# A normalisation, a projection and a state-space mixer whose instructions follow one order listed in the source

## The chip, the cores and the metric

The kernel runs on one NeuronCore of a Trainium2 chip. The core has five engines with a queue each: TensorE (PE in the profile), VectorE (DVE), ScalarE (ACT), GpSimd (POOL) and SyncE (SP), which here only starts transfers. An engine takes its instructions strictly in the order of its queue and stops at one whose inputs are not there yet. Transfers are started from SP, ACT and POOL. The metric is the device time of the whole kernel in microseconds (us); the median of the runs of a kernel is compared.

## The reference

The reference is a trunk of two layers on a sequence of 1024 vectors of 1024 elements (one sequence). Layer 0 mixes along the sequence with a diagonal state-space mixer (S5), layer 1 with a Mamba-2 mixer, and each mixer is followed by a squared-ReLU MLP. All is float32. Only the beginning of layer 0 is touched by the change:

```python
mod = cond @ ada_w[i] + ada_b[i]                   # cond = silu(c)
sh1, sc1, g1, sh2, sc2, g2 = jnp.split(mod[:, None, :], N_MOD, axis=-1)
h = _modulate(_rmsnorm(x, norm_mix_g[i]), sh1, sc1)   # norm * (1 + scale) + shift
# inside _s5_mixer:
u = (h @ w_in).astype(f32)                         # 1024 x 1024 by 1024 x 1024
bu = jnp.einsum('btgh,gph->btgp', u_blk, b_bar)    # 64 groups of 16 channels, 64 complex states
_, hs = lax.associative_scan(_s5_combine, (a_elems, bu), axis=1)
y = jnp.einsum('btgp,ghp->btgh', hs, c_mat).real
g = jax.nn.gelu(y + d * u)
val, gate = jnp.split(g @ w_glu + b_glu, 2, axis=-1)
x = x + g1 * (val * jax.nn.sigmoid(gate))
```

## The kernel before

Activations lie transposed: eight tiles of 128 channels (index k or m), each in two halves of 512 positions (index f). A float32 product in full precision is made of three float32r products (`mm3`, lines 118 to 120): of the high part of the weight with the high and the low part of the activation, and of the low part of the weight with the high part of the activation. So each weight unit of 128x1024 is loaded by SP into a tile `raw`, its high part is cast by ACT (`whi`, L85) and its low part is the difference, made by DVE (`wlo`, L86).

The part that the change touches is the first 270 us or so, in three steps.

**The first norm.** Eight loads bring x. ACT squares each half tile (`sq`, L196), PE sums the squares over channels in four strips of 32 rows of a bank (L184), DVE makes the inverse root (`rsqrt`). The scale is eight weighted sums on DVE (L403, each over a loaded tile `ada`), the shift is a product on PE (L381: one row of 512, eight terms after each other, for each half of the channels), which ACT copies out (L351), PE turns into columns (L354) and DVE stores as `mod` (L386). Then DVE scales each half tile (L1655), ACT adds the shift and rounds (L244) and DVE makes the low part (L245). Beside it DVE computes tables of powers and phases for the mixer (`s5_tables`).

**The input projection** (`s5_uproj`) makes u in eight blocks m of 128 channels, each in two halves. ACT copies each out to a tile `us` (L1098) in another order of positions, and for six of the eight blocks ACT writes it to DRAM and SP loads it back as the tile U (L1148). Blocks 6 and 7 go from `us` to U by eight transfers of 64 KB each (L1146).

**The mixer** works through the same eight blocks; a block is eight groups, worked in two quads (16 quads in all, called q below). `s5_front` and `s5_back` build the matrices of a block: DVE forms ET and Fa (L981, three instructions each per quad); PE makes the taps of a short convolution (L1028), which ACT copies into `kp`; POOL writes them skewed to DRAM by eight transfers (L1043) and loads them back as M (L1060), which ACT reorders (`Mp`, L1062); two transfers from POOL make Fb, which is Fa with its two halves of the partitions exchanged (L1065, L1066); PE transposes ET (L1073) and ACT copies it out as E; ACT and DVE make phases and ACT their sines (`si`, `co`, L1079 to L1088, with L1080 and L1081 on DVE). `s5_main` then takes a quad: PE multiplies U by E into two banks p1 and p2 (L1155, L1156); DVE turns them by the phase (three instructions, L1138), scans along the sequence (four, L1163) and turns back by two products, qa and qb (L1138); PE sums U by M, qa by Fa and qb by Fb in one bank (L1175, L1177); ACT applies GELU (`gy`, L1181) and starts its transfer to DRAM. `s5_gather` loads the result in tiles by channel and splits them into high and low parts (L1204, L1205). The gated linear unit (`glu`) takes these as its input; its first products are made while the mixer's last quads still run, and its first activation is `gt` (L1230).

The order on each engine is not written in the source: a scheduler orders the instructions by a priority, from the order of the program, and by a cost model, before the kernel runs. Tiles come from rings of buffers, and an instruction that takes a buffer waits until its last reader is done.

Of the kernel before, what the change touches and what calls it, by code (L numbers as in the profile page):

```python
# [19 lines left out]
P = 128  # L20
# [5 lines left out]
DIRECT = (6, 7)  # L26
# [156 lines left out]
def strip(K, bank, col, rows, k):  # L183
    K.nc.tensor.matmul(  # L184
        bank[blk(k % 4, 32)], col.to_broadcast([P, 32]), rows, start=k < 4, stop=k >= KT - 4, skip_group_check=True
    )


def rstd_first(K, x):

    nc = K.nc
    pr = [psw(K), psw(K)]
    for k in range(KT):
        for f in range(2):
            sq = tmp(K, "sq")
            nc.scalar.activation(sq, x[k][f], AF.Square)  # L196
            strip(K, pr[f], K.ones, sq, k)
    pt = columns(K, pr, K.heads)
    v = K.tmp.tile([P, 8], F32, tag="rfv", name="rfv")
    nc.vector.tensor_scalar(v, pt[:, 0:8], 1.0 / D, EPS, op0=ALU.mult, op1=ALU.add)  # L200
    y = K.tmp.tile([P, 8], F32, tag="rfy", name="rfy")
    rsqrt(K, y, v)
    return [spread(K, y[:, f * 4:f * 4 + 4], psw) for f in range(2)]
# [99 lines left out]
def mod_setup(K):  # L303
    nc = K.nc
    cc, tc = K.tmp.tile([P, 8], F32, tag="cc", name="cc"), K.tmp.tile([P, 8], F32, tag="ct", name="ct")
    nc.scalar.dma_start(cc, K.io.ccol)
    nc.scalar.activation(tc, cc, AF.Tanh, scale=0.5)
    K.condc = K.const.tile([P, 8], F32, name="condc")
    nc.vector.scalar_tensor_tensor(K.condc, tc, 1.0, cc, op0=ALU.add, op1=ALU.mult)
    K.mod = K.const.tile([P, 96], F32, name="mod")  # L310
    K.G = K.const.tile([P, 32], F32, name="G")

# [31 lines left out]
def columns(K, rows, heads=None):  # L344

    nc = K.nc
    pt = pss(K)
    for f, r in enumerate(rows):
        row = tmp(K, "row")
        n = P if heads else 1  # L350
        nc.scalar.copy(row[0:n], r[0:n])  # L351
        for j in range(4):
            o = pt[:, f * 4 + j:f * 4 + j + 1]
            nc.tensor.matmul(o, row[0:n, blk(j)], heads or K.ones[0:1], start=True, stop=True)  # L354
    return pt


def mod_first(K, units):


    nc, V, io = K.nc, K.nc.vector, K.io

    def tile():
        return K.adap.tile([P, 1024], F32, tag="ada", name="ada", bufs=K.nada)

    def blocks(f):
        ts = [tile().rearrange("p (k c) -> p k c", k=2) for _ in range(4)]
        for j, t in enumerate(ts):
            nc.sync.dma_start(t, io.ada0[2 * j:2 * j + 2, :, half_of(f)].rearrange("k p c -> p k c"))
        return ts  # L370

    def rows(f):
        ts = [tile() for _ in range(4)]
        for j, t in enumerate(ts):
            nc.sync.dma_start(t, io.ada[0, 8 + f * 4 + j])
        return ts

    def shift(f, ts):
        pr = pss(K)
        for k in range(KT):  # L380
            nc.tensor.matmul(  # L381
                pr[0:1], K.condc[:, k:k + 1], ts[k // 2][:, k % 2], start=k == 0, stop=k == KT - 1
            )
        pt = columns(K, [pr])
        o = C_ADAB + f * 4
        V.scalar_tensor_tensor(  # L386
# [3 lines left out]
    first = blocks(0), rows(0)  # L390
    units()
    gb, gh = [K.tmp.tile([P, 8], F32, tag=t, name=t, bufs=1) for t in ("fgb", "fgh")]
    g0 = K.cst[:, C_GMIX:C_GMIX + 8]
    V.scalar_tensor_tensor(gb, K.cst[:, C_ADAB + 8:C_ADAB + 16], 1.0, g0, op0=ALU.add, op1=ALU.mult)
    V.tensor_scalar(gh, g0, 0.5, None, op0=ALU.mult)
    acc = K.tmp.tile([P, 8], F32, tag="mac0", name="mac0", bufs=1)
    for f in range(2):
        bs, rs = (blocks(1), rows(1)) if f else first
        shift(f, bs)
        for j, r in enumerate(rs):  # L400
            k = f * 4 + j
            a = acc[:, k:k + 1]
            V.scalar_tensor_tensor(r, r, 1.0, K.cond, op0=ALU.mult, op1=ALU.mult, accum_out=a)  # L403
            nc.scalar.activation(
                K.G[:, k:k + 1], a, AF.Identity, scale=gh[:, k:k + 1], bias=gb[:, k:k + 1]
            )
            yield k
# [452 lines left out]
def s5_tables(K, keep, pool, Lm):  # L860
# [25 lines left out]
    V.memset(S.quarter, TWO_PI / 4)  # L886

# [4 lines left out]
    m1, em1 = exp_acc(K, pool, a, 64, minus_one=True)  # L892

# [34 lines left out]
    )  # L928
    S.R = []
    for nm in "12":  # L930
        r = keep.tile([P, 64, 9], F32, name="R" + nm, tag="R" + nm, bufs=1)
        u = pool.tile([P, 64, 9], F32, name="su", tag="su", bufs=1)
        sines(K, r, ph, *o[nm], u)
        V.tensor_tensor(r, r, mag, op=ALU.mult)
        S.R.append(r)

# [10 lines left out]
    V.tensor_tensor(s2, s2, s2, op=ALU.mult)  # L947
    V.tensor_tensor(s2, s2, m1, op=ALU.mult)
    V.scalar_tensor_tensor(nr, s2, -2.0, em1, op0=ALU.mult, op1=ALU.add)
    V.tensor_tensor(ni, ni, m1, op=ALU.mult)  # L950
    den, t = T("den"), T("dent")
    V.tensor_tensor(den, re, re, op=ALU.mult)
    V.tensor_tensor(t, im, im, op=ALU.mult)
    V.tensor_tensor(den, den, t, op=ALU.add)
# [17 lines left out]
    return S  # L972


def s5_front(K, S, pool, outp, m):


    nc, V, io = K.nc, K.nc.vector, K.io
# [951 lines left out]
```

## Time and profile before

| what | value |
|---|---|
| median of 3 runs | 2464.45 us (2461.76 to 2466.18) |
| the profiled execution | 2460.05 us |
| its span | 2458.3 us |
| busy share of the span: PE, DVE, ACT, POOL | 97%, 77%, 48%, 10% |
| start of the last GELU of the mixer | 258.52 us |
| start of the first activation of the gated unit (`gt`) | 271.26 us |

In the profile an engine's busy time is the time in which at least one of its instructions ran; idle time stands with what ended it. Instructions of one engine overlap by a little: the next one starts before the last one is over, so what an instruction costs its engine is the distance from start to start, and this is shorter than its duration. A line number is that of the kernel before unless the text says otherwise. The change ends with the first part of the gated unit: from there to the end both kernels have the same instructions in the same order on each engine.

### The profile page before, as it was taken

What the parts mean: (1) busy time and instruction counts of PE and PEld (TensorE: products, weight loads), DVE (VectorE), ACT (ScalarE), POOL (GpSimd) and SP (SyncE); (2) the same over time, 40 slices, a digit from 0 to 9 for tenths busy, and PEclk for the clock granted to TensorE, in tenths of its full rate; (3) what the DMA queues carried; (4) which work ended last, traced back from release to release, by engine and by line L of the source; (5) the groups of instructions that cost most, each with busy time, mean ns of one, the idle gap of its engine ahead of it and who ended that gap; (6) DMA issues with size and microseconds to landing.
All of it is one profiled execution on the core that took longest, in us unless ns stands there. A gap on an engine that the chain in (4) does not pass through costs nothing.

```text
span 2458.3 us, 32615 instructions
## 1 busy us (share of the span) xinstructions
PE 2396.3 (97%) x11496; PEld 1941.5 (79%) x11496; DVE 1893.7 (77%) x3205; ACT 1173.9 (48%) x1999; POOL 250.9 (10%) x468
## 2 busy tenths in 40 slices
PE   7899999999999899999999999999999999999997
PEld 2688888888788688878877777877888888888886
DVE  6998755968878997867695867789688788687665
ACT  4688313744444344534564655534147444454442
POOL 0232000122221000000000000000011222210000
PEclk9999999999999999999999999999999999999998
DMA  7566861567869999723454554674236677694752
GB/s 259 156 192 166 285 212 60 193 205 267 278 218 354 322 320 314 252 86 130 138 163 152 159 167 144 185 245 139 88 125 201 223 243 258 246 327 159 262 191 87
DMA packets 286260, 502.23 MB, mean 204 GB/s; under 512 B 23345, under 2 KB 163153, under 8 KB 286097
## 3 DMA queue, kind: packets, MB, share of 16 engines
q1 hardware_dynamic: 242336, 384.64, 49.0%
q0 software_dynamic: 33536, 107.90, 12.4%
q10 hardware_dynamic: 10224, 7.62, 1.0%
q8 instruction: 90, 1.47, 0.2%
q14 instruction: 74, 0.60, 0.1%
HBM read 362.71 MB, written 131.60 MB: 201 GB/s over the span
## 4 chain that ended last, share of the span: by engine, by line
PE 71%; issue 12%; DMA 6%; DVE 6%; ACT 3%; POOL 2%; DVEq 0%; SPq 0%; POOLq 0%; ACTq 0%
PE pd L119 8%; PE pd L118 8%; PE pd L120 8%; PE py L119 4%; PE py L120 4%; PE py L118 4%; PE px L118 3%; PE px L119 3%; PE px L120 3%; PE pv L118 2%; PE pv L119 2%; PE pv L120 2%; DMA ada<-in_ada 2%; PE pm L118 2%; PE pm L120 2%
## 5 line engine op out<-in xcount | busy, mean ns | idle before, releaser
L85 ACT CAST whi<-raw 128x1024 fp32r<-128x1024 f32 x241 | 251.3, 1048 | 417.6 <-PE pd L119 142.6
L86 DVE TENSOR_TENSOR wlo<-raw,whi 128x1024 fp32r<-128x1024 f32 x241 | 293.3, 1218 | 127.0 <-ACT whi L85 123.5
L341 DVE SCALAR_TENSOR_TENSOR ada<-ada,cond 128x1024 f32<-128x1024 f32 x80 | 97.5, 1223 | 44.1 <-DMA ada<-in_ada 43.9
L434 POOL DMA_DIRECT2D hscr<-x x32 | 17.4, 542 | 952.3 <-DVE x L815 753.5
L542 ACT ACTIVATE s<-s 128x512 f32<-128x512 f32 x84 | 53.1, 633 | 96.8 <-DVE s L540 95.3
L1361 DVE SCALAR_TENSOR_TENSOR cacc<-cr,conv,cacc 128x1024 f32<-128x1024 f32 x72 | 91.9, 1280 | 0.8 <-ACT cacc L1342 0.6
L1414 ACT ACTIVATE L<-csb,cs 128x128 f32<-128x128 f32 x224 | 69.9, 391 | 40.9 <-DMA csb<-csr 40.8
L549 POOL DMA_DIRECT2D b<-s x96 | 51.9, 541 | 277.8 <-ACT s L543 263.8
L549 POOL DMA_DIRECT2D b<-tt x96 | 51.9, 541 | 34.1 <-DVE tt L554 24.2
L543 ACT ACTIVATE s<-s 128x512 f32<-128x512 f32 x84 | 53.2, 633 | 2.7
L540 DVE TENSOR_TENSOR s<-s,px 128x512 f32<-128x512 f32 x60 | 40.9, 681 | 16.7 <-PE px L120 16.7
L1365 ACT ACTIVATE cth<-cacc 128x512 f32<-128x512 f32 x48 | 27.7, 625 | 42.0 <-DVE cacc L1361 40.0
L730 DVE SCALAR_TENSOR_TENSOR x<-py,mod,x 128x512 f32<-128x512 f32 x40 | 27.8, 746 | 23.6 <-PE py L120 23.6
L1043 POOL DMA_DIRECT2D kscr<-kp x64 | 34.4, 546 | 99.9 <-ACT kp L1034 98.4
L1230 ACT ACTIVATE gt<-pd,bgh 128x512 f32<-128x512 f32 x16 | 11.0, 686 | 67.9 <-PE pd L120 40.1
L118 PE MATMUL pd<-h00h,whi 128*128 128x512 f32 (+1 forms) x97 | 39.8, 412 | 2.8 <-ACT whi L85 2.8
L1434 DVE SCALAR_TENSOR_TENSOR y<-xs,cst,pm 128x128 f32<-128x128 f32 x128 | 38.3, 342 | 4.8 <-PE pm L1431 4.8
L1341 ACT COPY cr<-pd 128x512 f32<-128x512 f32 x48 | 27.8, 580 | 28.5 <-PE pd L120 28.5
L120 PE MATMUL pd<-h00h,wlo 128*128 128x512 f32 (+1 forms) x97 | 38.6, 398 | 2.8 <-DVE wlo L86 2.8
L215 ACT ACTIVATE sq<-x 128x512 f32<-128x512 f32 x28 | 16.8, 625 | 50.6 <-DVE x L730 45.6
L118 PE MATMUL pd<-h01h,whi 128*128 128x512 f32 x97 | 39.5, 408 | 0.8 <-DVE h61h L815 0.6
L554 DVE TENSOR_TENSOR tt<-s,b 128x512 f32<-128x512 f32 x56 | 38.6, 690 | 0.8
(1017 smaller groups left out, 8122.7 us busy)
## 6 DMA issues: line engine op xcount, KB each, us to landing
raw<-in_w SPq DMA_DIRECT2D x204, 512.0 KB, 4.8
br<-b SPq DMA_DIRECT2D x112, 512.0 KB, 5.7
ada<-in_ada SPq DMA_DIRECT2D x96, 512.0 KB, 5.0
b<-s POOLq DMA_DIRECT2D x96, 256.0 KB, 4.5
b<-tt POOLq DMA_DIRECT2D x96, 256.0 KB, 4.8
csb<-csr SPq DMA_DIRECT2D x32, 512.0 KB, 4.6
raw<-in_w_xbc SPq DMA_DIRECT2D x24, 512.0 KB, 4.3
xscr<-cacc SPq DMA_DIRECT2D x24, 512.0 KB, 2.7
```

Of the source, the lines that this page charges most:

```text
L85: K.nc.scalar.copy(hi, src)
L86: K.nc.vector.tensor_tensor(lo, src, hi.bitcast(F32), op=ALU.subtract)
L118: K.nc.tensor.matmul(ps, wh, xh, start=start and i == 0, stop=False, skip_group_check=more)
L119: K.nc.tensor.matmul(ps, wh, xl, start=False, stop=False, skip_group_check=more)
L120: K.nc.tensor.matmul(ps, wl, xh, start=False, stop=stop and i == n - 1, skip_group_check=more)
L341: K.nc.vector.scalar_tensor_tensor(r, r, 1.0, K.cond, op0=ALU.mult, op1=ALU.mult, accum_out=acc)
L540: nc.vector.tensor_tensor(t, t, p, op=ALU.add)
L542: nc.scalar.activation(t, t, AF.Relu)
L543: nc.scalar.activation(t, t, AF.Square)
L549: self.K.nc.gpsimd.dma_start(self.bscr[DOWN.index(nm)][m // 2][m % 2], t)
L1361: V.scalar_tensor_tensor(acc, cr[:, t:t + L], K.cw[:, i, t:t + 1], acc, op0=ALU.mult, op1=ALU.add)
L1414: nc.scalar.activation(Lm[:, r, :], cb[:, r, :], AF.Relu, bias=S.cs[:, c0 + r:c0 + r + 1], scale=-1.0)
```

## The change

The text of the program for these three steps is cut into some 600 small steps with names such as `A.3` (the product of U and E for quad 3), and a table in the source lists them in one order. Inside that stretch the scheduler is told to keep the order in which the steps are written, on all five engines. So each engine's queue is the list with the other engines' steps left out. Besides:

- The sums of squares and the shift's product both go through four strips of 32 columns and are summed by a product with a column that has a one at the head of each strip (`Strips`). Before, the shift's product was one row of 512.
- The products of the power table with the magnitudes, and the small chain that makes the tables q, move from DVE to POOL; qx moves from DVE to ACT.
- The rounding of the phase (L1080 on DVE) becomes a second run of eight activations on ACT with a bias (`pk`).
- The diagonal term is made once on POOL, and added to the taps by one small instruction of POOL per block (`tap0`). ACT copies all eight taps.
- Instead of Fb and a product with it, qb is added to qa with its two halves of partitions exchanged by two transfers from POOL that accumulate (`added`), and one product with Fa follows. Block 7 keeps Fa, Fb and two products, with Fb made by SP.
- U is filled straight from `us` for all blocks, by eight transfers from SP; DRAM is no longer used for it. The skewed writes of the taps, the loading back of M, the writes of the GELU's result and half of the last quads' transfers move to SP.
- Three of the gathered tiles are loaded into buffers of the mixer that have become free.

```diff
+ORDER = """
+x.0 lam cst x.3 x.7 x.6 cr tb.0 x.4 sq.0.1 tb.1 sq.0.0 x.1 sq.7.0 cc cnd rw.1.2 sq.3.0 x.5 tb.2 x.2 sq.6.0
...
+Fx.5 hi.4 sw.1 Ex.4 Fy.4 ul.2.0 T.3 ia.3 Fy.5 ml.1 Fz.4 To.3 Fz.5 pr.3.1.0 tp.4 tp.5 cd.2 ou.0 to.4 Ey.4 lo.4
+ib.3 to.5 sn.2 Ez.4 bc.4 pr.3.0.1 Ex.5 A.3 ic.3 pk.2 t0.2 Ey.5 ph.2 cx.2 fi.3 pr.3.1.1 cy.2 B.1 ca.3 di.1 tu.2
...
+class Strips:
+    def add(self, col, rows, strip):
+        n = self.n[strip] = self.n.get(strip, 0) + 1
+        self.K.nc.tensor.matmul(
+            self.bank[blk(strip, 32)], col.to_broadcast([P, 32]), rows, start=n == 1, stop=n == 2,
+            skip_group_check=True,
+        )
...
+    for r in S.R:
+        G.tensor_tensor(r, r, mag, op=ALU.mult)
...
+    def tap0(self, m):
+        kp = self.o[m].kp
+        self.nc.gpsimd.tensor_tensor(kp[:, :, 0], kp[:, :, 0], self.S.dI[:, 2 * m:2 * m + 2], op=ALU.add)
...
+    def skew(self, m):
+        for g in range(8):
...
+            self.nc.sync.dma_start(skew, src.unsqueeze(1).to_broadcast([16, 8, 128]))
...
+    def U(self, m, half):
...
+        for g in range(half * 4, half * 4 + 4):
+            self.nc.sync.dma_start(b.U[:, g], us[blk(g, 16)])
...
+    def added(self, q):
+        qa, qb = self.r["q", q]
+        for i in range(2):
+            self.nc.gpsimd.dma_start(qa[blk(i, 64)], qb[blk(1 - i, 64)], accum_op=ALU.add)
...
+        pairs = ((b.Fa, qa), (b.Fb, qb)) if m in TWO else ((b.Fa, qa),)
...
+    order = tc.manual_schedule(engines={E.PE, E.DVE, E.Activation, E.SP, E.Pool})
+    order.__enter__()
...
+    for step in ORDER.split():
+        name, *args = step.split(".")
+        do[name](*map(int, args))
+    order.__exit__(None, None, None)
```

In the table, `sn` is the scan of a quad, `cx` and `cy` are the two products that turn back, `sw` the two accumulating transfers, `B` the products into the bank that the GELU (`ou`) reads; `ul` fills half of a U, `sk` writes and `ml` loads the taps, `pr` is half of a projection's products.

How the queues move, first DVE in the norm. `mod` is the shift's columns, `ada` the weighted sums of the scale, `rfv` the start of the inverse root. Before:

```order
L403 SCALAR_TENSOR_TENSOR ada,mac_546<-ada,cond 128x1024 x2
L1655 SCALAR_TENSOR_TENSOR x_213<-x_213,G,pm 128x512
L1655 SCALAR_TENSOR_TENSOR x_214<-x_214,G,pm 128x512
L386 SCALAR_TENSOR_TENSOR mod<-pn,cst 128x4
L403 SCALAR_TENSOR_TENSOR ada,mac_546<-ada,cond 128x1024
L245 SCALAR_TENSOR_TENSOR h00l<-x_213,mod,h00h 128x512
```

and in the changed kernel:

```order
L467 SCALAR_TENSOR_TENSOR ada,mac_254<-ada,cond 128x1024 x3
L1018 TENSOR_SCALAR phik<-rt 128x64
L1019 TENSOR_SCALAR phik<-phik 128x64
L1020 SCALAR_TENSOR_TENSOR phi<-rt,phik 128x64
L1833 SCALAR_TENSOR_TENSOR x_215<-x_215,G,pm 128x512
L1833 SCALAR_TENSOR_TENSOR x_216<-x_216,G,pm 128x512
L1833 SCALAR_TENSOR_TENSOR x_213<-x_213,G,pm 128x512
L1833 SCALAR_TENSOR_TENSOR x_216<-x_216,G,pm 128x512
L1833 SCALAR_TENSOR_TENSOR x_214<-x_214,G,pm 128x512
L460 SCALAR_TENSOR_TENSOR mod<-pn,cst 128x4
```

The first `mod` now stands behind seven of the eight sums and five scaled half tiles, where it stood behind two of each.

Then PE at the first quad's last products (Mp is M reordered; pd is a bank of the projection). Before, at the start of the four groups:

```order
L119 MATMUL pd<-h50l,whi 128x512
L120 MATMUL pd<-h50h,wlo 128x512
L118 MATMUL pd<-h60h,whi 128x512
L1175 MATMUL pm<-U,Mp 128x128
L1177 MATMUL pm<-qa,Fa 128x127
L1177 MATMUL pm<-qb,Fb 128x127
```

and in the changed kernel, at the last of the four groups:

```order
L1256 MATMUL pm<-U,Mp 128x128
L1260 MATMUL pm<-qa,Fa 128x127
L1163 MATMUL pn<-ident,ET 128x128 x4
L160 MATMUL pd<-h01h,whi 128x512
L161 MATMUL pd<-h01l,whi 128x512
L162 MATMUL pd<-h01h,wlo 128x512
```

The product with Fb is gone, for 14 quads with four groups each: 56 products. In both kernels the projection's products stand between those of the quads.

Last SP, in the first blocks of the mixer. Before:

```order
L987 DMA BC<-in_s_bc 128x512 x2
L96 DMA raw<-in_s_w_in 128x1024
L1148 DMA U<-uscr 128x8x128
L987 DMA BC<-in_s_bc 128x512
L96 DMA raw<-in_s_w_in 128x1024
L1148 DMA U<-uscr 128x8x128
```

and in the changed kernel:

```order
L1205 DMA U<-us 128x1x128 x4
L1134 DMA kscr_77<-kp 16x8x128 x8
L1205 DMA U<-us 128x1x128 x4
L1140 DMA M<-kscr_77 128x8x128
L1276 DMA gscr<-gy 128x4x128
L1061 DMA BC<-in_s_bc 128x512
L138 DMA raw<-in_s_w_in 128x1024
L1134 DMA kscr_76<-kp 16x8x128 x8
```

A block has some three transfers on SP before (of U, BC and a weight unit) and 21 in the changed kernel, in one queue.

More of the change, by code (lines that the diff above doesn't have):

```diff
@@ L180, in rstd_half, with __init__, add, row @@
     return spread(K, y, bank)
[L183 to L203, printed above, removed]
+class Squares:
+    def __init__(self, K, x):
+        self.K, self.x, self.s = K, x, {}
+    def add(self, k, f):
+        K = self.K
+        if f not in self.s:
+            self.s[f] = Strips(K, psw(K))
+        sq = tmp(K, "sq")
+        K.nc.scalar.activation(sq, self.x[k][f], AF.Square)
+        self.s[f].add(K.ones, sq, k % 4)
+    def row(self, f):
+        self.s[f].row()
+    def columns(self, f):
+        if f == 0:
+            self.pt = pss(self.K)
+        self.s[f].columns(self.pt[:, f * 4:f * 4 + 4])
+    def rstd(self):
+        K, V = self.K, self.K.nc.vector
+        v = K.tmp.tile([P, 8], F32, tag="rfv", name="rfv")
+        V.tensor_scalar(v, self.pt[:, 0:8], 1.0 / D, EPS, op0=ALU.mult, op1=ALU.add)
+        y = K.tmp.tile([P, 8], F32, tag="rfy", name="rfy")
+        rsqrt(K, y, v)
+        return y
 def norm_steps(K, x, half, each, bank, order):
@@ L341, in mod_dot @@
     K.nc.vector.scalar_tensor_tensor(r, r, 1.0, K.cond, op0=ALU.mult, op1=ALU.mult, accum_out=acc)
[L344 to L351, printed above, removed]
-        for j in range(4):
[L353 to L384, printed above, removed]
@@ L385, in shift @@
         o = C_ADAB + f * 4
-        V.scalar_tensor_tensor(
+        K.nc.vector.scalar_tensor_tensor(
             K.mod[:, f * 4:f * 4 + 4], pt[:, 0:4], 0.5, K.cst[:, o:o + 4], op0=ALU.mult, op1=ALU.add
         )
[L390 to L407, printed above, removed]
+    def scale(self, k):
+        K, r = self.K, self.r[k]
+        a = self.acc[:, k:k + 1]
+        K.nc.vector.scalar_tensor_tensor(r, r, 1.0, K.cond, op0=ALU.mult, op1=ALU.mult, accum_out=a)
+        K.nc.scalar.activation(
+            K.G[:, k:k + 1], a, AF.Identity, scale=self.gh[:, k:k + 1], bias=self.gb[:, k:k + 1]
+        )
@@ L886, in s5_tables @@
     V.memset(S.quarter, TWO_PI / 4)
+    S.magic = KT_("magic", 1)
+    V.memset(S.magic, MAGIC)
+    S.d, S.one16, S.dI = KT_("s5d", 16), KT_("one16", 16), keep.tile([P, 16, 16], F32, name="dI", tag="dI", bufs=1)
+    S.dd = T("s5dd")
+    G = nc.gpsimd
+    G.memset(S.dd, 0.0)
+    yield S
     dt = exp_acc(K, pool, ld, 64)
@@ new lines, in phase, with turns @@
+    def phase(self, m, turns):
+        S, b = self.S, self.o[m]
+        t = self.G([P, 8, 128], "su" if turns else "tph")
+        if turns:
+            b.u = t
+        else:
+            b.t = t
+        for g in range(8):
+            self.nc.scalar.activation(
+                t[:, g, :], S.iota[:, 0:128], AF.Identity, scale=S.phi[:, m * 8 + g:m * 8 + g + 1],
+                bias=S.magic if turns else 0.0,
+            )
+    def turns(self, m):
+        b = self.o[m]
+        self.V.scalar_tensor_tensor(b.u, b.u, MAGIC, b.t, op0=ALU.subtract, op1=ALU.subtract)
@@ new lines, in table, with rst, feed, diagonal @@
+    def table(n):
+        r = next(tables)
+        if n == 0:
+            st.S = r
+    def rst():
+        st.y = squares.rstd()
+    def feed():
+        for g in range(4):
+            nc.sync.dma_start(st.S.dd[32 * g:32 * g + 16], io.s5_d)
+    def diagonal():
+        S, G = st.S, nc.gpsimd
+        for g in range(4):
+            strip, own = blk(g, 32), slice(32 * g, 32 * g + 16)
+            G.tensor_copy(S.d[strip], S.dd[strip, g:61 + g:4])
+            G.tensor_copy(S.one16[strip], K.ident[strip, own])
+        sh = [P, 16, 16]
+        G.tensor_tensor(
+            S.dI, S.one16.unsqueeze(1).to_broadcast(sh), S.d.unsqueeze(2).to_broadcast(sh), op=ALU.mult
+        )
```

697 lines of the change are left out of this document (411 added, 286 removed).

## The prediction

> **What bounds the kernel now.** I read the windows first, cut at three moments: the end of the last low part of the first norm on DVE (first row of the second fence), 218, from where DVE waits more often, and the start of `gt`, the gated unit's first activation (its second row).
>
> ```profile
> core 0: us, PE busy (x) PEld busy (x) DVE busy (x) ACT busy (x) POOL busy (x), PEclk, DMA share, GB/s
> 0.00:30.00 30.00, 18.56 (x54) 5.31 (x55) 18.80 (x109) 16.55 (x27) 5.11 (x19) 1.00 0.90 328
> 30.00:71.50 41.50, 36.04 (x128) 18.72 (x127) 33.80 (x57) 18.56 (x32) 0.00 (x0) 0.92 0.43 159
> 71.50:100.00 28.50, 24.77 (x145) 18.50 (x143) 23.68 (x47) 20.40 (x46) 12.00 (x21) 1.00 0.73 198
> 100.00:218.00 118.00, 114.53 (x803) 98.31 (x804) 115.90 (x227) 96.42 (x162) 32.57 (x56) 1.00 0.65 170
> 218.00:271.30 53.30, 49.28 (x301) 43.43 (x300) 38.59 (x63) 36.01 (x56) 6.18 (x11) 0.97 0.78 212
> 271.30:400.00 128.70, 128.70 (x569) 106.59 (x568) 67.82 (x118) 21.95 (x26) 7.06 (x13) 1.00 0.62 210
> ```
> ```profile
> 70.86 0.75 DVE L245 SCALAR_TENSOR_TENSOR h71l<-x,mod,h71h 128x512 fp32r<-128x512 f32 x1
> 271.26 0.69 ACT L1230 ACTIVATE gt<-pd,bgh 128x512 f32<-128x512 f32 x1 [3.40 <-PE pd L120]
> ```
>
> From 271.3 on PE is busy all the time, so what the change can win is how much earlier `gt` starts; it is carried to the end one for one, since the instructions behind it are the same. Two stretches lie before. In the norm (0 to 71.5) DVE is busy 18.80+33.80 = 52.6 us and waits for the rest. In the mixer (71.5 to 271.3, 199.8 us) PE is busy 24.77+114.53+49.28 = 188.6 us and DVE 23.68+115.90+38.59 = 178.2 us: two engines close to full, PE idle for 11.2 us.
>
> **The norm.** The waits of DVE there:
>
> ```profile
> engine line waited for: us in total, times, longest us
> DVE mod L386 <- PE pn L354: 7.3, 2, 4.0
> DVE rfv L200 <- PE pn L354: 3.3, 1, 3.3
> DVE ea_xc L830 <- DMA lam<-in_lam: 2.6, 1, 2.6
> DVE bgh L1638 <- DMA cst<-in_cst: 2.1, 1, 2.1
> DVE cond L300 <- ACT cond L299: 1.5, 1, 1.5
> 45.03 8.82 PE L381 MATMUL pn<-ada,condc 128*1 128x512 f32 x16
> ```
>
> The 7.3 us are the two halves of the shift, whose sixteen instructions for the second half take 8.82 us on PE (the last row; eight products, at a mean clock of 0.92 in that window). In the list the first `mod` stands behind seven weighted sums and five scaled tiles, the inverse root behind four sums, and the constants behind both exponentials. Each of these waits (7.3+3.3+2.1+1.5 = 14.2 us) then has work of DVE in front of it. The wait for `lam` stays, since the exponentials begin with it, and its transfer now stands second on ACT. Work also leaves DVE:
>
> ```profile
> L934 DVE TENSOR_TENSOR R<-R,mag 128x576 f32<-128x576 f32 x2 | 1.4, 747 | 0.0
> 21.23 0.21 DVE L960 TENSOR_TENSOR qt<-ni,lam 128x64 f32<-128x64 f32 x1
> 21.37 0.21 DVE L959 TENSOR_TENSOR q<-ni,lam 128x64 f32<-128x64 f32 x1
> 9.59 1.00 DVE L838 SCALAR_TENSOR_TENSOR ea_p<-ea_p,ea_r 128x64 f32<-128x64 f32 x4
> ```
>
> R is 1.4 us; fourteen small instructions at 0.14 us from start to start (21.23 to 21.37) are 1.9. Against that, the two exponentials now stand one behind the other; a chain of dependent instructions costs 0.25 each (1.00 us for four) where mixed ones cost 0.14, so some 35 of them lose up to 3.9; I take 2, since half of them stood in a chain before too. Sum: 71.5 - 14.2 - 3.3 + 2 = 56. The loads set another floor. In the first 30 us they ran at 328 GB/s, and what the norm needs is 27 transfers of 512 KB (x, c, the two kinds of `ada`, two units), 14.2 MB or 43 us; the last one to matter for the shift is about the 24th, at 38 us. The second `mod` stands behind some 46 us of work, so this floor is hidden, with little to spare. I take 60.5 for the end of the norm, **a gain of 11 us**, between 6 (half of the waits come back) and 15.
>
> **The mixer on PE.** The product with Fb is left out for 14 quads of four groups.
>
> ```profile
> 249.20 0.39 PE L1175 MATMUL pm<-U,Mp 128*128 128x128 f32 x2
> 249.42 0.39 PE L1177 MATMUL pm<-qa,Fa 128*128 128x127 f32 x2
> 249.65 0.39 PE L1177 MATMUL pm<-qb,Fb 128*128 128x127 f32 x2
> 251.51 0.39 PE L119 MATMUL pd<-h10l,whi 128*128 128x512 f32 x1
> 251.74 0.40 PE L120 MATMUL pd<-h10h,wlo 128*128 128x512 f32 x1
> 0.00:71.50 71.50, 18.66 (x69) 0.95 0.63 230
> ```
>
> From start to start such a product costs 0.22 us, so 56 are **12.4 us less** on PE. But PE begins this stretch with less done: the last row (PE on the tile `pd`) counts 69 products of the projection by 71.5, and in the list only four half projections, 48 products, stand ahead of the end of the norm. The 21 others, 0.23 us each, move behind it: **4.8 us more**. The strips that replace the shift's row lie in the norm, where the second `mod` has time: I price them at nothing.
>
> If PE were idle as long as now, the mixer would take 199.8 - 12.4 + 4.8 = 192.2 us. The idle 11.2 us are what a better order can win. Their causes:
>
> ```profile
> DVE qa L1138 <- PE pm L1155: 7.4, 3, 6.3
> ACT us L1098 <- PE pd L120: 10.0, 7, 3.2
> ```
>
> They are chains from engine to engine, the longest a DVE that stands still for 6.3 us until PE has made p1, and an ACT that waits for the projection. The list spreads the sixteen quads evenly: by the table, `A` of a quad stands well ahead of `ca`, and matrix work of the next blocks between. I take **5 us less**, between all 11.2 gone and 8 more.
>
> **The mixer on the others.** DVE loses L1080, the diagonal and the first tap.
>
> ```profile
> 206.20 0.67 DVE L1080 TENSOR_SCALAR su<-tph 128x1024 f32<-128x1024 f32 x1
> 206.78 0.69 DVE L1138 TENSOR_TENSOR qa<-qb,co 128x512 f32<-128x512 f32 x1
> L981 DVE TENSOR_TENSOR kp<-dI,pn 128x16 f32<-128x16 f32 x16 | 2.6, 164 | 3.4 <-PE pn L1028 3.2
> 226.48 1.28 ACT L1079 ACTIVATE tph<-iota,phi 128x128 f32<-128x128 f32 x4
> L1181 ACT ACT_TABLE_LOAD x11 | 14.1, 1283 | 0.2
> L1087 ACT ACT_TABLE_LOAD x7 | 9.0, 1283 | 0.1
> ```
>
> That is 8 x 0.58 + 2.6 = 7.2 us of DVE (171 left of 178), which is under what PE needs and so is worth nothing by itself. ACT gets 64 more activations of 0.32 us (1.28 for four), 20 us. Its tables of functions are loaded 22 times in this stretch (11 and 7 in these rows, four more at L1088) and in the changed queue 11 times, which gives back 14 us; the transfers that leave ACT give back more. ACT was busy 152.8 of 199.8 us and stays at about that, under PE.
>
> Of the transfers, the accumulating ones are new on the path: after `cy` of a quad, POOL starts two, and the quad's `B` on PE waits for both.
>
> ```profile
> Fb<-Fa POOLq DMA_DIRECT2D x16, 256.0 KB, 5.8
> kscr<-kp POOLq DMA_DIRECT2D x64, 64.0 KB, 3.2
> L1065 POOL DMA_DIRECT2D Fb<-Fa x8: 520/544/847, 85.6 to 223.5; - x8
> L1146 SPq DMA_DIRECT2D U<-us x16: 551/640/2357, 202.2 to 231.3; - x16
> 202.20 8.52 SPq L1146 DMA_DIRECT2D U<-us  x8
> ```
>
> No row shows an accumulating transfer. The nearest moves between halves of SBUF from the same queue (Fb, twice the bytes): 5.8 us to landing, plus 2 x 0.54 to start two, so 6.9 us. In the table `B` of a quad stands right behind `cy` of the next (`cy.2 B.1`), about one quad's period later; 188 us for 16 quads are some 11 us. It is hidden with 4 us to spare: cost 0, and if it took twice 5.8, 14 x 1.7 = 24 us. SP gets 21 starts per block; at the median 0.64 us of a U that is 13 of some 23 us, so its queue is not full: 0, and up to 20 in all if starts bunch as in the last row (1.07 each).
>
> **Sum.** -11 - 12.4 + 4.8 - 5 = -23.6 us. On the profiled execution, 2460.05, this is 2436.5; the median of the runs lies 4.4 above it, so **2441 us**. Its own range, from the bounds of the norm (6 to 15) and of PE's idle time (-11.2 to +8): 2431 to 2458.
>
> One rule speaks against the moves to POOL. The Trainium skill, "SBUF — State Buffer", section "Who interferes with whom", has it that a VectorE instruction with two SBUF inputs and a GpSimd instruction that reads SBUF exclude each other, and the later one waits for the whole of the earlier. No row before shows two such instructions at once, so the profile neither confirms nor denies it; what it would make of the sum stands among the rivals, from rows.
>
> **The rivals.**
>
> *PE's idle time goes entirely, and the norm gains its most:* 2464.45 - 15 - 12.4 + 4.8 - 11.2 = 2431, or a little less with a clock of 1.00 for 0.97 in the last stretch: 2428. For it: the sums of DVE and ACT lie under PE's. Against it: an order fixed beforehand cannot react to a transfer that is late.
>
> *SP's queue holds the mixer up.* U, the taps, M, the GELU's results and the units stand in one queue, each waiting for its producer, and `ml` waits at its head until the eight `sk` have landed. At 1.07 us a start, and 8 + 3.2 us for the taps, each block would be late by some 2.5 us: +20, 2460, no change. Against it: the mean of 0.64.
>
> *The accumulating transfer is late (the other side).* It decides from the point where a landing takes more than some 9.9 us (11 less the two starts). At 14 us from `cy` to landed data with the starts, 3 us on each of 14 quads, 42 us: 2483, slower. For it: the transfer reads and adds where a plain one writes. Against it: half the bytes of Fb, which landed in 5.8.
>
> *DVE is locked out while POOL works.* A copy of 32x16 on POOL took 0.33 us (first row below) where DVE's 128x16 above took 0.16: twice. The moved work, 3.3 us of the norm and 2.6 of the mixer, would be 12 us on POOL; if DVE stood still for all of it, the norm would lose 6.6 us: 2448.
>
> ```profile
> L970 POOL COPY s5d<-s5dd 32x16 f32<-32x16 f32 x4 | 1.3, 329 | 15.8 <-DMA s5dd<-in_s_d 15.8
> ```
>
> This is what the rule above would give.
>
> **How the numbers follow.** Chances: the forecast 0.58, no idle time 0.12, SP 0.12, the late accumulation 0.10, the lock 0.08. A difference under 0.2% (4.9 us) cannot be told from no change. The forecast, the case without idle time and the lock are faster, and of the SP case a third: 0.81; the rest of the SP case and a forecast at its edge are the same: 0.08; the late accumulation and a badly held queue are slower: 0.11. The range for 8 in 10 goes from 2426, a little beyond the best case, to 2464, which takes in the SP case and leaves out the late accumulation.
>
> **What would show it.** Right: the norm's last low part ends on DVE near 60 us, DVE's waits for `mod` nearly gone; `gt` starts near 248; PE shows 16 records with Fb instead of 128 and less than 10 us idle in the mixer; the accumulating transfers land within 6 us and no `B` waits for them for long; ACT shows 11 loads of tables behind the norm. Wrong: PE waiting for qa at the new line of `B` in most quads (accumulation); SP's own waits over 100 us together with PE or ACT waiting for U or M (SP); DVE instructions of 1.2 us where 0.69 stood, beside POOL's products (lock); or a `gt` that is early and a gated unit with idle PE behind it.

## The result, and the profile after

The changed kernel takes 2438.59 us (median of 5 runs, 2435.89 to 2446.64) where the kernel before took 2463.84 on the same chip: a ratio of 0.9907, with a 95% interval from 0.9886 to 0.9928, or 25 us less. The forecast was 2441, in a range from 2426 to 2464.

Windows of the changed kernel, cut at the end of the norm and at the start of `gt` (columns as in the prediction's first fence):

```profile
0.00:62.90 62.90, 44.57 (x167) 23.08 (x168) 55.23 (x152) 31.97 (x56) 18.70 (x35) 0.84 0.77 278
62.90:243.90 181.00, 174.92 (x1144) 149.77 (x1143) 166.65 (x298) 161.65 (x318) 34.93 (x40) 0.98 0.78 175
```

The timeline rows that set these cuts, the last low part of the norm on DVE and the first `gt` on ACT:

```profile
62.14 0.74 DVE L1841 SCALAR_TENSOR_TENSOR h51l<-x,mod,h51h 128x512 fp32r<-128x512 f32 x1
243.92 0.67 ACT L1365 ACTIVATE gt<-pd,bgh 128x512 f32<-128x512 f32 x1
```

`gt` starts 27.3 us earlier than before (271.26). The norm gave 8.6 of it (71.5 to 62.9), the mixer 18.8 (199.8 to 181.0). In the mixer PE is busy 174.9 us and idle 6.1; DVE (166.7) and ACT (161.7) lie close below.

What PE still waited for in the mixer (us in total, times, longest), the group of the product with Fb, and the accumulating transfers (count, size, median us to landing):

```profile
PE pm L1213 <- ACT E L1169: 2.5, 1, 2.5
PE pm L1213 <- DMA U<-us: 1.8, 2, 1.2
PE pm L1213 <- DVE h00l L1340: 0.7, 1, 0.7
PE pm L1256 <- DVE qa L1051: 0.5, 1, 0.5
L1260 PE MATMUL pm<-qb,Fb 128*128 128x127 f32 x16 | 3.1, 275 | 0.0
qa<-qb POOLq DMA_DIRECT2D x28, 128.0 KB, 3.6
```

No product waited for an accumulating transfer. Of the products with Fb 16 records are left of 128; a product leaves two records, so these are 8 products of 64.

For the experiments one mark is better than the first `gt`: the last `gt` of the gated unit, since PE is full from one to the other and the mark is the same instruction in every kernel. It stands at 426.54 before (one execution), and in three profiled executions of the changed kernel at 400.22, 399.67 and 401.65, on average 400.51. All gains and losses below are counted from that 400.5; a spread of 2 us belongs to it. From the first `gt` to this mark it is 155.3 us before and 156.3 to 156.6 in the changed kernel: about 1 us of the 27.3 belongs to the first mark and is no gain.

### The profile page after: what moved, and what is told of

The parts are those of the page before. It is cut to its first block, busy times and chain, and to the rows that moved or that the text cites. A ratio compares the mean times of both kernels' runs of the same rounds, so it can differ in the third digit from the quotient of the medians.

```text
span 2440.6 us, 32530 instructions
## 1 busy us (share of the span) xinstructions
PE 2378.4 (97%) x11384; PEld 1936.0 (79%) x11384; DVE 1890.3 (77%) x3158; ACT 1181.3 (48%) x2053; POOL 248.8 (10%) x436
## 3 DMA queue, kind: packets, MB, share of 16 engines
q0 software_dynamic: 31424, 99.25, 11.2%
## 4 chain that ended last, share of the span: by engine, by line
PE 77%; issue 7%; DMA 6%; DVE 5%; ACT 4%; POOL 2%; SPq 0%; DVEq 0%; POOLq 0%; ACTq 0%
PE pd L160 11%; PE pd L162 11%; PE pd L161 11%; PE py L162 4%; PE py L161 4%; PE py L160 4%; PE px L160 3%; PE px L162 3%; PE px L161 3%; PE pm L160 2%; PE pv L160 2%; PE pm L162 2%; PE pm L161 2%; PE pv L162 2%; PE pv L161 2%
## 5 line engine op out<-in xcount | busy, mean ns | idle before, releaser
L127 ACT CAST whi<-raw 128x1024 fp32r<-128x1024 f32 x231 | 241.4, 1048 | 426.3 <-PE pd L161 146.0
L128 DVE TENSOR_TENSOR wlo<-raw,whi 128x1024 fp32r<-128x1024 f32 x231 | 281.0, 1218 | 122.0 <-ACT whi L127 118.3
L793 DVE SCALAR_TENSOR_TENSOR x<-py,mod,x 128x512 f32<-128x512 f32 x40 | 27.8, 743 | 23.6 <-PE py L162 23.6
L161 PE MATMUL pd<-h00l,whi 128*128 128x512 f32 (+1 forms) x97 | 38.9, 401 | 0.0
L1521 DVE TENSOR_TENSOR L<-L,cm 128x1024 f32<-128x1024 f32 x32 | 38.9, 1215 | 0.0
```

What stands on the lines that cost most here:

```text
L127: K.nc.scalar.copy(hi, src)
L128: K.nc.vector.tensor_tensor(lo, src, hi.bitcast(F32), op=ALU.subtract)
L161: K.nc.tensor.matmul(ps, wh, xl, start=False, stop=False, skip_group_check=more)
```

## The experiments

**The order alone.** The first experiment keeps every part of the change and takes the listed order (715 entries) away; the second keeps the order only up to the end of the norm.

```diff
-    order = tc.manual_schedule(engines={E.PE, E.DVE, E.Activation, E.SP, E.Pool})
-    order.__enter__()
...
-    order.__exit__(None, None, None)
```

> All parts of the change stay, and the 600 steps are still written in the order of the table, but the scheduler orders each engine's queue as it did before. Theory (the order brings what the prediction put on it: the waits of the norm, 8.6 us as measured, and 5 of idle time of PE): `gt` starts near 257.5, the time is some 13 us above the changed kernel's, 2452. Rival: the order is worth nothing, since fewer products, fewer loads of tables and moved transfers carry the gain: `gt` within 3 us of 243.9, time 2439 to 2442. A third: this code suits the scheduler worse than the old code did: over 2464.

```diff
     for step in ORDER.split():
+        if step == "bar":
+            order.__exit__(None, None, None)
...
-    order.__exit__(None, None, None)
```

> The listed order holds only up to the end of the norm (the step `bar`); the mixer behind it is ordered by the scheduler, from the same steps. The kernel without any listed order ended its norm at 77.4 and started `gt` at 276.3; the changed kernel at 62.9 and 243.9. Theory (both halves of the order carry): the norm ends near 63, the mixer takes as long as without the order (198.9 us, PE idle for some 18 of them), so `gt` near 262 and the time 2451 to 2455. Rival: the early norm is lost again in the mixer without its order (it waits for transfers or for DVE), `gt` at 270 or later, about as before. Rival 2: the mixer was slow only because of the late norm, `gt` under 250.

Without the order the time is 2466.19, beside 2465.15 of the kernel before (ratio 1.0012, 0.9998 to 1.0026): the whole gain is gone, as the third case of its expectation had it (over 2464). The last `gt` stands at 431.55, 31.0 us later than in the changed kernel and 5.0 later than before. With the order in the norm alone it is 2453.37 (0.9952, 0.9938 to 0.9967) and the last `gt` at 416.06. So the order of the norm is worth 15.5 us and that of the mixer another 15.5. The windows without any order:

```profile
0.00:77.40 77.40, 51.22 (x167) 25.42 (x168) 50.57 (x152) 34.29 (x58) 18.11 (x35) 0.71 0.63 226
77.40:276.30 198.90, 180.98 (x1149) 151.23 (x1148) 167.91 (x300) 164.82 (x321) 36.29 (x40) 0.97 0.73 163
```

and of the mixer with the norm ordered:

```profile
63.00:260.80 197.80, 180.12 (x1145) 150.90 (x1144) 167.75 (x299) 164.86 (x321) 36.14 (x40) 0.97 0.73 163
```

In the mixer without its order PE is busy 181.0 us, 7.6 less than the 188.6 of the kernel before: near the 9.2 of the product with Fb less the 14 products of the projection that come later (12.4 - 3.2; 55 stand ahead of the end of the norm here, 69 before). But it is idle for 17.9 us instead of 11.2, and 6.7 of the 7.6 are gone again. The waits that did it, first of DVE in the norm without any order:

```profile
DVE rfv L249 <- PE pn L415: 14.1, 1, 14.1
```

and of PE in the mixer with the norm ordered:

```profile
PE pn L1163 <- DVE ET L1051: 4.5, 2, 3.8
PE pn L1113 <- DVE Fa L1051: 3.2, 2, 2.8
PE pn L1163 <- ACT kp L1123: 2.4, 1, 2.4
```

The scheduler put work of DVE behind the inverse root that could have stood in front of it, and DVE stood still for 14.1 us. In the mixer PE stood at transposes and taps whose inputs were not made yet. With the norm ordered the mixer took nearly as long as without (197.8 and 198.9): the early norm is neither lost nor does it cure the mixer. The theory of the second run is borne out (forecast for `gt` near 262, measured 260.8); that of the first had the direction, but 13 us where 24 (the medians of that set) to 31 (the last `gt`) were measured.

**The product with Fb.** It is put back for all quads, inside the same order; Fb is made for each quad by two transfers from POOL.

```diff
-TWO = (7,)
+TWO = tuple(range(8))
...
+        b.Fb[q] = self.O([P, 4, 16, 8], "Fb", 2)
+        for i in range(2):
+            self.nc.gpsimd.dma_start(b.Fb[q][blk(i, 64)], b.Fa[blk(1 - i, 64), o])
```

> The product with Fb is put back for all blocks (two more products for each pair of groups, Fb made by two transfers for each quad from POOL, as many starts as the accumulating ones had), and the accumulating transfers are gone. Theory (PE bounds the mixer): 56 products more at 0.22 us, `gt` 12.4 us later, near 256, time +12. Rival 1: DVE and ACT, each busy for 97 to 98% of the stretch from 62.9 to 200, bound it, and PE has room: +0 to +4. Rival 2: the accumulating transfers cost waits of their own, which go away here: between +4 and +9, with the idle time of PE under 4 us where the changed kernel has 6.1.

```profile
63.00:256.20 193.20, 185.86 (x1257) 161.32 (x1256) 166.79 (x299) 161.29 (x317) 28.21 (x44) 0.99 0.69 161
```

The last `gt` is at 412.83, 12.3 us later, where the theory had 12.4. PE is busy 10.9 us longer, and it is idle for 7.3 us where it was 6.1. DVE and ACT have the same work in 12 us more. PE bounds the ordered mixer. The median is 2448.55 (0.9942, 0.9919 to 0.9965), 6.5 above the changed kernel's of the same set (2442.04); the smaller difference lies behind the gated unit and is told of in the last experiment.

**Work moved between DVE, ACT and POOL.** The rounding of the phase goes back from ACT to DVE; in another kernel the two products R go back from POOL to DVE; a third has both.

```diff
-        G.tensor_tensor(r, r, mag, op=ALU.mult)
+        V.tensor_tensor(r, r, mag, op=ALU.mult)
...
     def phase(self, m, turns):
         S, b = self.S, self.o[m]
+        if turns:
+            return
...
+        b.u = self.G([P, 8, 128], "su")
+        self.V.tensor_scalar(b.u, b.t, MAGIC, None, op0=ALU.add)
         self.V.scalar_tensor_tensor(b.u, b.u, MAGIC, b.t, op0=ALU.subtract, op1=ALU.subtract)
```

> The rounding of the phase goes back from ACT (64 activations, 20 us) to DVE (8 instructions, 8 x 0.58 = 4.6 us), directly before the instruction that uses it. From 62.9 to 200 all three engines are nearly full in the changed kernel: PE 133.5, DVE 133.3 and ACT 133.9 of 137.1 us. Theory (PE bounds, as forecast: this move is worth nothing by itself): `gt` within 1.5 us of 243.9. Rival ACT (its chains set the pace): 3 to 6 us earlier. Rival DVE (it sets the pace): 4 to 5 us later.

```profile
62.80:245.30 182.50, 173.18 (x1140) 147.75 (x1139) 171.75 (x306) 138.70 (x254) 34.48 (x40) 0.99 0.79 174
```

ACT loses 23 us of its 161.7 and DVE gains 5.1, and the last `gt` moves to 401.63, 1.1 us later, inside the spread of the changed kernel. Neither ACT nor DVE sets the pace up to this mark: the move is worth nothing there, as the prediction had it. The median is 2435.78, 6.3 below the changed kernel's of the same set (2442.04); that difference lies behind the gated unit and is taken up in the last experiment.

> Only the two products of the power table (R, 128x576) go back from POOL to DVE. In the changed kernel an instruction of DVE took 1.66 us (su, 128x576) beside the first of them and another 1.38 us (rfy, 128x8) beside the second, where the like of it took 0.51 and 0.17. Theory (the two engines exclude each other there): these two are 0.51 and 0.17 again, 2.4 us come back, the two products cost 2 x 0.67 on DVE: the norm ends 1.0 us earlier, near 61.9, and `gt` 1 us earlier. Rival (they were long for another reason): both stay, the norm ends 1.4 us later, near 64.3. In either case the time cannot be told from that of the changed kernel, and the profile decides.

The rows of the changed kernel, DVE first and then POOL, start and duration in us:

```profile
27.91 1.66 DVE L918 TENSOR_SCALAR su<-ph,o 128x576 f32<-128x576 f32 x1
31.29 1.38 DVE L186 SCALAR_TENSOR_TENSOR rfy<-rst,rsi 128x8 f32<-128x8 f32 x1
...
27.08 2.17 POOL L1014 TENSOR_TENSOR R<-R,mag 128x576 f32<-128x576 f32 x1 [25.46 <-ACT R L920]
31.25 1.40 POOL L1014 TENSOR_TENSOR R<-R,mag 128x576 f32<-128x576 f32 x1 [2.00 <-ACT R L920]
```

and with R on DVE:

```profile
28.07 0.52 DVE L918 TENSOR_SCALAR su<-ph,o 128x576 f32<-128x576 f32 x1
30.31 0.17 DVE L186 SCALAR_TENSOR_TENSOR rfy<-rst,rsi 128x8 f32<-128x8 f32 x1
35.03 1.42 DVE L1014 TENSOR_TENSOR R<-R,mag 128x576 f32<-128x576 f32 x2
```

The two long rows are gone: each had ended right behind R on POOL (29.57 behind 29.25, 32.67 behind 32.65), so DVE had stood still for it. This agrees with the Trainium skill, "SBUF — State Buffer", section "Who interferes with whom", by which the later of the two waits for the whole of the earlier. Of the two only rfy reads two tensors; su, which reads one, was held as well, so the case is wider here than the prediction put it. But the norm ends at 62.66 instead of 62.88, not 1.0 us earlier. POOL's chain for the tables q starts earlier in this kernel and meets more of DVE's low parts: between 44 and 54 us nine instructions of DVE are 0.03 to 0.37 us longer than they are alone, 0.9 us in all, where the changed kernel has 0.3. The exclusion is shown; its net price in the norm, 0.2 us, is under what these marks can tell, and the last `gt` (400.89) stays where it was. The median is 2435.37, in a set without the changed kernel.

> R and the rounding of the phase both back on DVE, all else as changed. Alone they gave 2435.4 and 2435.8, against 2438.6 and 2442.0 of the changed kernel, though the gated unit ended 0.7 and 1.4 us later. Theory (their moves are worth nothing, the difference is chance behind the mixer): the gated unit ends 1 to 3 us later than in the changed kernel and the median lies within 4 us of it. Rival (DVE does both at no cost, and relieving ACT and POOL helps): faster than the changed kernel by over 4 us.

Both together: 2437.67, beside 2437.62 of the changed kernel in the same set; the last `gt` is at 401.46. In this set there is no gain and no loss.

**The cover of the accumulating transfers.** A small copy that reads qb and 15 or 60 memsets stand ahead of the two transfers of each quad on POOL.

```diff
         qa, qb = self.r["q", q]
+        self.nc.gpsimd.tensor_copy(self.K.ssq, qb[:, 0:32])
+        for i in range(15):
+            self.nc.gpsimd.memset(self.K.ssq, 0.0)
         for i in range(2):
             self.nc.gpsimd.dma_start(qa[blk(i, 64)], qb[blk(1 - i, 64)], accum_op=ALU.add)
```

> Ahead of the two accumulating transfers of each of the 14 quads POOL gets one small copy that reads qb and fifteen small memsets, so that they start some 2 to 4 us after their data are there (the trace gives the delay d). In the changed kernel the product that needs them starts 6.6 to 14.4 us after the first of the two starts, which land within 4.6 to 5.3: a cover of 1.5 to 9 us. Theory (hidden): `gt` 0 to 6 us later. Rival (the transfers are on the path already): 14 x d, some 40 us later.

> The same with sixty memsets, d some 6 to 12 us. Theory: the cover is used up in nearly all quads, and PE, whose queue is fixed, waits for what is over: 14 x (d - 3.5), for d = 9 some 75 us, `gt` near 320. Rival: later quads have more room than that, since everything in front of them shifts too: under 30 us.

The wait of PE for these transfers with 15 memsets:

```profile
PE pm L1263 <- DMA qa<-qb: 9.7, 6, 5.2
```

the same with 60:

```profile
PE pm L1263 <- DMA qa<-qb: 60.6, 12, 8.8
```

and, with 15, the timeline of the quad that waited longest, on POOL and then on PE:

```profile
131.99 4.15 POOL L1245 COPY ssq<-qb 128x32 f32<-128x32 f32 x1 [4.68 <-DVE qb L1051]
136.21 2.67 POOL L1247 MEMSET ssq<- 128x32 f32 x15
139.28 1.67 POOL L1249 DMA_DIRECT2D qa<-qb  x2 [0.40 <-issue]
147.55 0.77 PE L1263 MATMUL pm<-qa,Fa 128*128 128x127 f32 x2 [5.21 <-DMA qa<-qb]
```

With 15 memsets the delay was 2.9 us for the first quad and 7.3 for the one shown, whose copy took 4.15 us instead of 0.21 (DVE was in a run of two-input products). Six of 14 quads waited, 9.7 us in all; their transfers started 3.5 to 7.4 us after qb was ready, where it is 0.3 to 0.5 in the changed kernel. The last `gt` came at 412.51, 12.0 later: twice the 0 to 6 expected, but far from the 14 times d of the rival. The median is 2447.04 (0.9933, 0.9916 to 0.9949).

With 60 memsets the last `gt` stands at 476.27, 75.8 later, and the median is 2508.27 (1.0183, 1.0167 to 1.0199): slower than before. The delay is 11.1 us for the first quad (86.35 to 97.41), but it grows: from qb to the first start it is 11.1 to 22.2 us, 15.7 on average. POOL itself falls behind, since copy, memsets and starts take it some 13 us per quad, and quads come every 10 us in the changed kernel. Rows of POOL, one quad's work close behind the other's:

```profile
194.06 1.59 POOL L1245 COPY ssq<-qb 128x32 f32<-128x32 f32 x1
195.71 10.86 POOL L1247 MEMSET ssq<- 128x32 f32 x60
206.95 1.65 POOL L1249 DMA_DIRECT2D qa<-qb  x2 [0.39 <-issue]
208.21 0.81 POOL L1245 COPY ssq<-qb 128x32 f32<-128x32 f32 x1
```

So this run shows that a large delay is paid for, but the loss cannot be turned into a cover per quad, and that the 75 us of the expectation came out is luck: by its formula a delay of 15.7 would have cost 14 x (15.7 - 3.5) = 171 us.

The cover can be read from the changed kernel itself, as the time from the landing of a quad's second transfer to the product that needs it: 5.0 us on average over the 14 quads, 12.4 at most, and 0.2 at the tightest. In the tightest the second transfer started at 166.85 and landed 7.0 us later, at 173.81 (the last row has the landing of its two transfers, min/median/max):

```profile
166.29 1.67 POOL L1246 DMA_DIRECT2D qa<-qb  x2 [4.94 <-DVE qb L1051]
174.00 0.40 PE L1260 MATMUL pm<-qa,Fa 128*128 128x127 f32 x2
DMA to landing us min/median/max: 2.8/4.9/7.0
```

In the two further executions of the changed kernel the smallest cover is 1.2 and 2.2 us.

The other side of the same question is block 7, which kept Fb. Here it accumulates too:

```diff
-TWO = (7,)
+TWO = ()
...
-cx.14 cy.14 bg.1.3 B.14 cy.15 ou.14 B.15
+cx.14 cy.14 sw.14 bg.1.3 B.14 cy.15 sw.15 ou.14 B.15
```

> Block 7 accumulates too: Fb and its product are gone for all 16 quads, two more quads have accumulating transfers, started right behind `cy.14` and `cy.15`, and the products that need them follow at once, with only six products of the gated unit between. Eight products fewer are 1.8 us. Theory (a landing of 4.6 to 5.3 us with the starts, with no cover here): PE waits some 4 us for quad 14 and 1 for quad 15, and runs slow for a short time after; `gt` 3 to 5 us later. Rival (the landing is hidden here too): `gt` 1.8 us earlier.

```profile
227.20 3.34 POOL L1246 DMA_DIRECT2D qa<-qb  x4 [10.72 <-issue]
235.10 0.77 PE L1260 MATMUL pm<-qa,Fa 128*128 128x127 f32 x2 [6.72 <-DMA qa<-qb]
```

The four transfers start behind each other, and the first quad's product runs 7.9 us after the first start; PE waits 6.7 us (4 and 1 expected for the two quads). The last `gt` is at 407.92, 7.4 later (3 to 5 expected), and the time is 2443.19 (0.9916, 0.9901 to 0.9932). Where nothing stands between, the two accumulating pairs cost 7.4 us and save eight products, 1.8 us.

**What happens behind the gated unit.** There the changed kernel gave back part of its lead. Two more runs of it, and one with a single additional memset at the beginning:

> The changed kernel once more, nothing edited. In its first profiled execution `gt` started 27.3 us earlier than before (243.92 for 271.26), but the piece behind it, whose instructions are the same in both kernels, took 2196.7 us (2440.6 - 243.9) where before had 2187.0 (2458.3 - 271.3). Theory: these 9.7 us are what one execution differs from the next by; this run shows `gt` at 243.9 within 1 us again and a piece behind it nearer to 2190, and the time stays between 2435 and 2447. Rival: the change makes the later part slower in a regular way; then the piece is 2196 to 2198 again.

> The changed kernel a third time, beside the three others on one chip. In its two executions so far the end of the gated unit came 26.3 and 26.9 us earlier than before, but the end of the kernel only 18.1 and 17.7: 8 to 9 us lost behind it, at waits for transfers after which the granted clock dips. In the kernel with R on DVE the loss was 1.3 us, in the one with the rounding on DVE -0.6. Theory (chance of the execution): a loss anywhere from -1 to 9. Rival (this very program has the later part slower each time): 8 to 9 again, and the median 4 to 7 us above that of the kernel with both moves back on DVE.

> The changed kernel with one memset of 128x32 more on POOL at its very beginning, and nothing else. Theory: nothing that can be told, the median within 3 us of the changed kernel's in this set, the end of the gated unit 26 to 27 us before that of the kernel before. Rival (where the later part is slow is decided by when its transfers start, to a fraction of a microsecond, so that any nudge moves it): the same end of the gated unit, but a later part shorter by 4 us or more.

```diff
     make_identity(nc, K.ident)
+    nc.gpsimd.memset(K.ssq, 0.0)
```

From the last `gt` to the end of the span it took 2031.8 us before, 2040.4, 2040.8 and 2037.4 in the three executions of the changed kernel, 2031.0 with the memset, 2033.0 with R on DVE, 2031.2 with the rounding on DVE, and between 2030.5 and 2037.2 in the other kernels, all with the same instructions. The instructions of ACT behind the mark are the same 1633 in the same order in all of them. Run times show the spread within one kernel: with the memset the profiled execution took 2433.11 and the four others 2439.75 to 2442.09; the third run of the changed kernel took 2440.67 in its profiled execution and 2433.49 to 2440.22 in the others. So a later part shorter by 6 to 10 us, which the rival of the memset forecast and its one profile shows, is not a property of that kernel, and about 10 us are what one execution differs from the next by. The second run, taken alone, spoke for its rival (a later part that is slow each time), and the medians of the last set (2437.62, with the memset 2440.40, with both moves back 2437.67) speak against it. Whether a few us belong to the changed kernel all the same stays open: its three profiled executions have the longest later parts of all, and over all sets its 14 runs have a median of 2439.8, the 13 runs with R, the rounding or both on DVE 2435.6. One place where time is lost can be seen. The first product at this place waits for a sum on DVE whose input was loaded back from DRAM; the row is of the kernel with the rounding on DVE:

```profile
486.40 0.50 PE L160 MATMUL px<-h01h,whi 128*128 128x512 f32 x1 [1.11 <-DVE s L596]
```

and this one of the changed kernel:

```profile
486.07 0.50 PE L160 MATMUL px<-h01h,whi 128*128 128x512 f32 x1 [2.22 <-DVE s L596]
```

These windows follow in the changed kernel (the clock granted to PE is the third column from the right):

```profile
486.00:488.00 2.00, 1.93 (x7) 1.60 (x8) 0.61 (x2) 0.00 (x0) 0.00 (x0) 0.84 0.12 44
488.00:490.00 2.00, 2.00 (x6) 1.54 (x6) 0.00 (x0) 0.00 (x0) 0.00 (x0) 0.50 0.00 0
490.00:492.00 2.00, 2.00 (x9) 1.60 (x8) 0.69 (x1) 0.69 (x2) 0.00 (x0) 0.80 0.00 0
492.00:494.00 2.00, 2.00 (x11) 1.64 (x10) 0.51 (x1) 1.09 (x2) 0.54 (x1) 1.00 0.03 12
```

and this one behind the shorter wait, with the rounding on DVE:

```profile
488.00:490.00 2.00, 2.00 (x11) 1.63 (x10) 0.53 (x1) 0.00 (x0) 0.00 (x0) 1.00 0.01 5
```

The transfer landed 1.1 us later, the wait was 2.2 instead of 1.1, and then the clock was halved for some 3.6 us, which cost 1.6 us more. The lead fell here by 2.7 us (from 26.3 to 23.6) in the one execution, and by nothing in the other. This place alone does not make the difference: the two other executions of the changed kernel have the same dip behind waits of 1.9 and 2.6 us, and so has the kernel with R on DVE (2.4), whose later part is 2033.0 all the same. In the changed kernel's first execution the loss goes on growing until some 840 us. Which transfers land late in an execution, and why, was not tried.

## Why the prediction was right

The time was met within 2.4 us, and most steps hold one by one; the share that the prediction gave to the order was too small by half, and that the time came out so near is in part luck, since errors of the sum cancelled.

**The norm.** Forecast 60.5, measured 62.9. All the waits that were to go are gone (DVE waits in the norm for nothing but `lam`). The constants came in time, and both `mod` stood behind enough work. But the terms of the prediction add up to 56; the 4.5 us up to 60.5 were a margin without a row, and the norm ended 6.9 us behind its sum. 1.6 of these are the wait that the prediction kept: `lam` landed later, the exponentials start at 6.61 us instead of 4.99. Some 2.7 are the exclusion with POOL (2.4 at the two R, 0.3 later), which had no term in the sum. The other 2.6 no run separates. The strips, priced at nothing, caused no wait for `mod`. The 8.6 us understate the order: with the new code the scheduler's norm ended at 77.4, so the order's own share is 14.5 there.

**The products.** The 12.4 us of Fb were measured as 12.3. Ahead of the end of the norm stood 55 products of the projection, not 48, so that term was +3.2 instead of +4.8.

**PE's idle time.** Forecast 6.2, measured 6.1; this agreement hides that the step was wrong in kind. The prediction subtracted 5 from the 11.2 of the old code, as if the parts and the order could be added. The new code under the scheduler idles for 17.9, so the order removes 11.8. Without it all the parts together, the 12.4 us of Fb among them, shortened the mixer by 0.9 us (199.8 to 198.9). The parts are worth something only with the order, and the order was worth 31 us with these parts; what it is worth with the parts of before was not tried. The prediction's case against a mixer without idle time, that an order fixed beforehand cannot react to a late transfer, holds for the scheduler's order as well, which is also fixed before the kernel runs.

**PE's busy time.** By the prediction's terms it should have been 188.6 - 12.4 + 4.8 = 181.0; it was 174.9. The two terms above explain 1.6 of these 6.1 us. Without the order in the mixer the same products took 180.1, so the rest, 4.5 us, comes with the order too. About 1 us of it is the first `gt`, which stands 1 us further ahead of the last one; how the others come about, these runs do not tell. It covered the 2.4 us of the norm, and `gt` came at 243.9 instead of near 248.

**The rest of the way.** That the start of `gt` is carried to the end one for one was right within 2 us (27.3 at the first `gt` with 1 us of it the mark's, 26.0 at the last `gt` on average, 25.3 in the medians), but one execution can differ by 10 us behind it; the profiled one lost 8.6.

**Costs of nothing.** SP: its queue waited for others for some 81 of the 181 us, and PE waited 1.8 us for U; that it had room is read from the trace and was not tried. ACT: 161.7 us busy for some 159 by the prediction's terms, 11 loads of tables as forecast, and giving 23 us back changed nothing. The accumulating transfers: landing 3.6 us (2.6 to 7.0) for 5.8 taken, hidden in all 14 quads. But "4 us to spare" was a mean period less a mean landing. Measured, the mean cover is 5.0 us and the smallest 0.2, so the run with 15 memsets already lost 12. The strips, the filling of U straight from `us` and the gathered tiles in other buffers were not taken out one by one.

**The rivals.** No idle time at all: not so, 6.1 us stayed. SP and the late accumulation: not so; the second is real from a delay of some 3.5 us on, and with 60 memsets, where POOL fell behind as well, the gain turned into a loss. The lock: the mechanism exists and took 2.4 us of DVE at the two R. The prediction found no row of it in the kernel before, but there is a likely one: the four POOL copies that it took as 0.33 us each took 0.46, 0.44, 0.21 and 0.21, and the second began within a two-input instruction of DVE (17.79 to 18.54) and ended right behind it, at 18.60. Its "twice" was thus a mean of unlike rows. In the mixer it is POOL that waits. Its product with 32 elements per partition took 0.25 us when DVE was not in its way and 2.11 when it was, while DVE's two-input products stayed at 0.68. The rival's 12 us of blocked DVE assumed that every instruction of POOL blocks DVE.

The rows, first that copy and the instruction of DVE before, then two of POOL's product in the changed kernel:

```profile
18.16 0.44 POOL L970 COPY s5d<-s5dd 32x16 f32<-32x16 f32 x1 [4.22 <-DMA s5dd<-in_s_d]
...
17.79 0.75 DVE L856 SCALAR_TENSOR_TENSOR su<-su,ph 128x576 f32<-128x576 f32 x1
...
72.94 0.25 POOL L1127 TENSOR_TENSOR kp<-kp,dI 128x32 f32<-128x32 f32 x1 [16.03 <-ACT kp L1123]
...
101.47 2.11 POOL L1127 TENSOR_TENSOR kp<-kp,dI 128x32 f32<-128x32 f32 x1 [5.93 <-ACT kp L1123]
```

## What to carry to other kernels

Work taken off the busiest engine pays only where its inputs are then ready earlier. Here the products with Fb cost 12.3 us under the listed order. Under the scheduler's order all parts of the change together, these products left out among them, shortened the mixer by only 0.9. So price a change together with the order that it will run in, not as a sum of both. Judge a hidden transfer by its tightest place and not by the mean: the mean cover was 5.0 us, the smallest 0.2, and a quad whose transfers started 3.5 us after its data already waited. Compare profiles at a mark soon behind the change, since the rest of the kernel can differ by 10 us from one execution to the next.

## What the runs showed of the hardware

- A wait of PE of 2.2 us was followed by 3.6 us at a granted clock of 0.50, beginning 1.3 us after PE had started again; one of 1.1 us at the same place was not (rows and windows above). Waits of 1.9, 2.4 and 2.6 us there in three other executions were followed by a clock of 0.50 to 0.52 over 2 us too. The Trainium skill, "TensorE: Matmul & The Clock Gate", section "HAM oscillation — how this bites in real kernels", warns of gaps over about 3.4 us. Here a shorter one was enough, and the measurement decides.
- A copy of 128x32 on POOL that took 0.21 us took 4.15 us while DVE ran two-input products back to back; DVE started six of them in that time. So a small instruction on POOL can lose several turns.
- Transfers between two places of SBUF that add to their target (128 KB, 64 partitions) landed in 3.6 us (median of 28, from 2.6 to 7.0), where plain ones of 256 KB took 5.8 in the kernel before.
